# The context's four recurrence steps between the decays of later pieces, with weights loaded together and the recurrence placed ahead

## The chip, the cores and the metric

The kernel runs on one core of one Trainium2 chip. The metric is the device time of one execution in microseconds (us), taken as the median of several runs.

## The reference, cut to what matters

One layer of a diffusion backbone. A context of 256 tokens and a latent stream of 1024 tokens go through the same combined projection; its columns feed a short gated convolution and a bidirectional RWKV-7 recurrence. The recurrence runs over the context first, in both directions, and the latents start from the states that the context left:

```python
def wkv_scan(state0, r, decay, kk, b, v, k, reverse):
    def step(S, inp):
        r_t, w_t, kk_t, b_t, v_t, k_t = inp
        sa = jnp.einsum("bhvk,bhk->bhv", S, kk_t)
        S = (S * w_t[:, :, None, :] - sa[..., None] * b_t[:, :, None, :]
             + v_t[..., None] * k_t[:, :, None, :])
        return S, jnp.einsum("bhvk,bhk->bhv", S, r_t)
...
        hc = modulate(rms_norm(ctx, norm1_g[l]), csh1, csc1)
        out_c, ctx_states = mixer_block(hc, lp, (zero_state, zero_state), not last)
        hx = modulate(rms_norm(x, norm1_g[l]), sh1, sc1)
        out_x, _ = mixer_block(hx, lp, ctx_states, True)
        x = x + g1 * out_x
        hx = modulate(rms_norm(x, norm2_g[l]), sh2, sc2)
        x = x + g2 * conv_ffn(hx, lp, rows, GRID_W)
```

`mixer_block` multiplies the concatenation of the two groups' outputs by `w_out`; the kernel splits this product into the convolution's half and the recurrence's half.

## The kernel before, in words

All work is in float32, with the large products done as three products of a rounded part (hi) and a rest (lo). The 1280 tokens are ten tiles of 128: tiles 0 and 1 are the context, 2 to 9 the latents. The program has these stages.

1. Norms, modulation and the projections of k and v, until about 270 us.
2. **Decays and inversions.** Five pieces of two tiles each, in the order 0 (the context), 2, 8, 4, 6 (`decay_and_invert`). The function `decays` handles a piece in eight groups (four blocks of channels j, two directions d). A group is two small products for the decays (`plo`), a row of operations on VectorE, ScalarE and GpSimd that make the factors `arO` and `kbO`, eight matrix multiplications into two banks `px` (L601 of before; they are recorded as sixteen, and are counted as sixteen below when rows are meant and as eight when the program is meant), VectorE's four masked reads of them (L603, L605), four transposes `pt`, and writes to DRAM. Then `invert` turns the piece's triangular blocks into their inverses: thirty pairs of dependent VectorE operations (L670, L672), two block transposes (L676, L678), 256 tiny products (`pq`, `pr`) and a write to DRAM (`xa_dram`, L700). The remaining projections (r, the gate, the convolution group: 17 columns of 48 matrix multiplications `pj`, L354) stand between this work on TensorE. Their weights are split by ScalarE and GpSimd (`wlo`, L106), and the convolution's own arithmetic (`cu`, `cy`, L832 to L840) is on VectorE.
3. **The recurrence.** `steps` does one chunk of 64 tokens of both directions. It loads the chunk (`cxa`, `ckb`, `car`, `cxr`, `vu`: 2.3 MB for both directions of a latent step), forms the right-hand side `ry` on TensorE (L752, L760), copies it to `rh` (L762, ScalarE for one direction, VectorE for the other), multiplies by the inverse into `pu` (L771), copies that to `vu` (L775, L777), multiplies into `ps` (L783), adds to the state `S` on VectorE (L786, four times) and, for latents, adds the outputs (L792, L800, L802). GpSimd multiplies the state and the loaded `car` by decays (L764, L650). Four steps cover the context, sixteen (r = 0 to 15) the latents. The latent step r takes tile 2 + r // 2 forward and tile 9 - r // 2 backward, so steps 0 to 3 need pieces 2 and 8 alone, and step 4 is the first that needs pieces 4 and 6.
4. **Work between the phases of a step.** `fill` takes parts from a list: `conv_out` (64 parts of three matrix multiplications, `pco`, L898) in latent steps 0 to 9, then per tile `mix`, `outp` (`po`, L898) and `to_h2`. The table `SL` says how many parts stand after each of the four phases of a step. `behind` holds these parts back until the recurrence's latest instructions are issued. `conv_out` needs `w_out`'s first four blocks, made by `w_make` (one product by the gate on VectorE, L891, a copy on ScalarE, a difference on GpSimd, L893).
5. The gated MLP, from about 1022 us to the end.

Each engine works off its instructions in the order that the program fixes; where the code leaves the order open, the framework's scheduler has chosen it at build time from its own model and from priorities. DMAs go out in order on SP's queue. PSUM's banks are handed out by `Banks`; a buffer or bank that is taken again makes the new user wait for the last reader of the old.

Of the kernel before, what the change touches and what calls it, by code (L numbers as in the profile page):

```python
# [2 lines left out]

# [12 lines left out]
D = 1024  # L16
# [13 lines left out]
SL = ((3, 2, 0, 2),) * 10 + ((0, 1, 3, 4),) + ((4, 4, 4, 6),) * 5  # L30
# [5 lines left out]
IB = 2  # L36
XB, XT = 2, 3
PADC, PADM = 88, 80
# [4 lines left out]
B1 = ((4, 5, 1), (2, 3), (6, 7), (0,), (1,))  # L43
# [4 lines left out]
B4 = dict(pm=(5, 7), px=(0,), ph=(4,))  # L48
# [39 lines left out]
def hybrid_kernel(  # L88
# [97 lines left out]
    md.tile([128, PADM], F32, name="padm")  # L186
# [327 lines left out]
    sx = ExitStack()  # L514
    dq = sx.enter_context(tc.tile_pool(name="dq", bufs=2, side="left", reuse_waits="tile"))
# [103 lines left out]

    Sd = []  # L620
# [4 lines left out]
    zero = st.tile([128, 2], F32, name="zero")  # L625
    G.memset(zero, 0.0)
    yts, before = {}, [None, None]

    class Chunk:


        def __init__(self, pool, d, t, ch):
# [13 lines left out]
            else:  # L646
                self.ar = pool.tile([128, 4, 2 * CH], F32, name="car")[:, :, 0:CH]
# [75 lines left out]
    def steps(pool, pairs, pp, bufs, sl=(0, 0, 0, 0)):  # L723


        cx = []
        rh = pool.tile([128, 512], F32, name="rh", bufs=1)
# [16 lines left out]
        for _ in cx:  # L744
            ry = pp.tile([128, 4, 128], F32, name="ry", tag="ry", bufs=bufs)
            rys.append((ry, ry.rearrange("p j (e v) -> p (j e) v", e=2)))
# [10 lines left out]
        for (u, v0, u0, vu, S), (ry, ry8) in both:  # L757
# [4 lines left out]
            chain["AV"[u.d]] = (A.copy, V.tensor_copy)[u.d](rh[u0:u0 + 64], ryf)  # L762
            if u.pc is not None:
                chain["G"] = F2.tensor_tensor(out=S, in0=S, in1=u.pc.to_broadcast([128, 4, 128]), op=ALU.mult)  # L764
        fill(sl[0])
        pus = [pp.tile([128, 4, 128], F32, name="pu", tag="pu", bufs=bufs) for _ in cx]
        with turns():
            for h in range(8):
                for (u, v0, u0, vu, S), pu in zip(cx, pus):
                    o = pu.rearrange("p j (e v) -> p (j e) v", e=2)[u0:u0 + 64, h, :]  # L770
                    chain["PE"] = PE.matmul(o, u.xa[u0:u0 + 64, h, :], rh[u0:u0 + 64, 64 * h:64 * h + 64], start=True, stop=True)  # L771
        for (u, v0, u0, vu, S), pu in zip(cx, pus):
# [3 lines left out]
            else:  # L776
                chain["V"] = V.tensor_scalar(out=vu[u0:u0 + 64], in0=puf, scalar1=-1.0, scalar2=None, op0=ALU.mult)  # L777
        fill(sl[1])
        for u, v0, u0, vu, S in cx:

            ps = pp.tile([128, 4, 64], F32, name="ps", tag="pu", bufs=bufs)
            for h in range(8):
                chain["PE"] = PE.matmul(ps[64 * (h % 2):64 * (h % 2) + 64, h // 2, :], u.kbt[:, 64 * h:64 * h + 64], vu[:, 64 * h:64 * h + 64], start=True, stop=True)  # L783
            for e in range(2):
                r = slice(64 * e, 64 * e + 64)
                chain["V"] = V.tensor_tensor(out=S[r, :, r], in0=ps[r], in1=S[r, :, r], op=ALU.add)  # L786
        fill(sl[2])
        both = [z for z in both if z[0][0].has_y]
# [4 lines left out]
        for (u, v0, u0, vu, S), (ry, ry8) in both:  # L793
# [10 lines left out]
            if e_[1] == 2 and (first or t in (3, 4)):  # L804
                SY.dma_start(yd[t], e_[0])
        fill(sl[3])

    ppc = Banks(px=B1[0], pj=B1[1], pl=B1[2], pq=B1[3], ry=B1[4], pu=B1[4])
# [36 lines left out]

    def decay_and_invert(ti):
# [22 lines left out]
    h2p = sh2.enter_context(tc.tile_pool(name="h2p", bufs=1, side="left", reuse_waits="tile"))  # L869
    h2 = [[h2p.tile([128, 8, 512], F32R, name=f"h2{hf}{i}", tag=f"h2{hf}{i}") for i in range(2)] for hf in range(1)]  # L870
# [12 lines left out]
    def w_raw(k):  # L883
        raws_[k] = cp_.tile([128, D], F32, name="xo", bufs=XB)
        SY.dma_start(raws_[k], w_out[0, 128 * k:128 * k + 128, :])

    def w_make(k):
# [5 lines left out]
        G.tensor_tensor(out=hl[1], in0=raw, in1=hl[0].bitcast(F32), op=ALU.subtract)  # L893
# [140 lines left out]
    ppc = Banks(ry=B2[0], pu=B2[1])  # L1034
    w_raw(0)
    w_raw(1)
    for r in range(4):
# [208 lines left out]
```

## Time and profile before

| | us |
|---|---|
| median of three runs | 1712.62 |
| the three runs | 1712.07, 1712.62, 1720.13 |
| the profiled execution, its own time | 1711.73 |
| its span in the trace | 1710.0 |

In the profiled execution TensorE's matrix multiplications are busy 91% of the span, VectorE 68%, ScalarE 33%, GpSimd 34%. TensorE's records overlap, so a full share means that it was never without work, not that it ran at its peak. The shares differ much by stage, so the argument goes by stretches of the trace. All times of rows are counted from the span's start.

### The profile page before, as it was taken

What the parts mean: (1) busy time and instruction counts of PE and PEld (TensorE: products, weight loads), DVE (VectorE), ACT (ScalarE), POOL (GpSimd) and SP (SyncE); (2) the same over time, 40 slices, a digit from 0 to 9 for tenths busy, and PEclk for the clock granted to TensorE, in tenths of its full rate; (3) what the DMA queues carried; (4) which work ended last, traced back from release to release, by engine and by line L of the source; (5) the groups of instructions that cost most, each with busy time, mean ns of one, the idle gap of its engine ahead of it and who ended that gap; (6) DMA issues with size and microseconds to landing.
All of it is one profiled execution on the core that took longest, in us unless ns stands there. A gap on an engine that the chain in (4) does not pass through costs nothing.

```text
span 1710.0 us, 27259 instructions
## 1 busy us (share of the span) xinstructions
PE 1558.9 (91%) x10639; PEld 1260.8 (74%) x10639; DVE 1157.2 (68%) x1795; ACT 565.1 (33%) x994; POOL 578.4 (34%) x515
## 2 busy tenths in 40 slices
PE   7699999989899966799678889999999999999997
PEld 2588768867777756687566768888888888788886
DVE  4963525698999987444578777777777777446645
ACT  2654315544445323221123421211111111324323
POOL 2343312333343304533344422222222222545643
PEclk9799799998999875999789999999999999999999
DMA  9385527557576486988652311111111111533531
GB/s 311 113 281 178 180 76 219 160 154 243 173 236 214 127 256 208 320 248 274 214 164 73 116 49 49 50 46 45 46 50 50 50 49 50 172 112 123 165 95 61
DMA packets 233721, 247.97 MB, mean 145 GB/s; under 512 B 18547, under 2 KB 171720, under 8 KB 233592
## 3 DMA queue, kind: packets, MB, share of 16 engines
q1 hardware_dynamic: 233208, 246.07, 46.2%
q8 instruction: 84, 1.38, 0.3%
q14 instruction: 45, 0.37, 0.1%
q0 software_dynamic: 384, 0.15, 0.0%
HBM read 179.32 MB, written 66.85 MB: 144 GB/s over the span
## 4 chain that ended last, share of the span: by engine, by line
PE 64%; DVE 23%; DMA 6%; ACT 3%; issue 3%; SPq 1%; POOL 0%; DVEq 0%; ACTq 0%
PE pf L1099 26%; PE pf L1179 13%; PE pj L354 10%; DVE tmp L670 3%; DVE ti L672 3%; PE pco L898 2%; PE po L898 2%; DMA araw<-in_ada_w_dram 2%; DVE acc L1146 2%; PE ry L760 1%; DVE xrO L605 1%; PE ry L752 1%; DVE xa L603 1%; PE ps L783 1%; PE px L601 1%
## 5 line engine op out<-in xcount | busy, mean ns | idle before, releaser
L1099 PE MATMUL pf<-h,fhi 128*128 128x512 f32 x1408 | 385.9, 391 | 5.9 <-DVE act L1151 4.1
L1099 PEld LDWEIGHTS pf<-h,fhi 128*128 128x128 f32 x1408 | 265.7, 189 | 62.6 <-DVE act L1151 4.5
L354 PE MATMUL pj<-hx,whi 128*128 128x512 f32 (+1 forms) x976 | 302.5, 389 | 1.6 <-DVE hx L328 1.3
L1146 DVE SCALAR_TENSOR_TENSOR acc<-gp,prm,acc 128x1024 f32<-128x1024 f32 x176 | 273.0, 1553 | 6.0
L106 POOL TENSOR_TENSOR flo<-fraw,fhi 128x1024 fp32r<-128x1024 f32 x50 | 122.0, 2441 | 315.8 <-ACT fhi L105 315.8
L1099 PE MATMUL pf<-h,flo 128*128 128x512 f32 x704 | 224.9, 392 | 0.0
L354 PEld LDWEIGHTS pj<-hx,whi 128*128 128x128 f32 x976 | 184.6, 197 | 38.2 <-issue 4.4
L354 PE MATMUL pj<-hx,wlo 128*128 128x512 f32 (+1 forms) x488 | 189.5, 389 | 0.0
L1179 PE MATMUL pf<-dhi,ahl 128*128 128x512 f32 x640 | 163.0, 389 | 0.2 <-DVE ahl L1171 0.2
L1171 DVE TENSOR_TENSOR ahl<-act,ahl 128x512 fp32r<-128x512 f32 x44 | 86.2, 1969 | 101.5 <-ACT ahl L1170 101.5
L1099 PEld LDWEIGHTS pf<-h,flo 128*128 128x128 f32 x704 | 132.9, 189 | 27.7 <-POOL flo L106 0.2
L105 ACT CAST fhi<-fraw 128x1024 fp32r<-128x1024 f32 x50 | 52.6, 1053 | 265.8 <-issue 158.4
L1179 PEld LDWEIGHTS pf<-dhi,ahl 128*128 128x128 f32 x640 | 120.0, 188 | 25.5 <-DVE ahl L1171 0.6
L106 POOL TENSOR_TENSOR dlo<-fraw,dhi 128x1024 fp32r<-128x1024 f32 x40 | 98.5, 2467 | 93.7 <-ACT dhi L105 89.7
L106 POOL TENSOR_TENSOR wlo<-wraw,whi 128x1024 fp32r<-128x1024 f32 x26 | 63.2, 2431 | 165.1 <-ACT whi L105 165.0
L1144 DVE TENSOR_SCALAR acc<-gp,prm 128x1024 f32<-128x1024 f32 x22 | 42.6, 1938 | 98.2 <-ACT gp L1136 98.2
L354 PEld LDWEIGHTS pj<-hx,wlo 128*128 128x128 f32 x488 | 96.2, 197 | 17.3 <-issue 1.7
L1179 PE MATMUL pf<-dlo,ahl 128*128 128x512 f32 x320 | 89.1, 389 | 0.0
L601 PE MATMUL px<-arO,kbO 64*128 64x128 f32 (+1 forms) x640 | 64.1, 308 | 18.3 <-DVE xrO L605 12.5
L601 PEld LDWEIGHTS px<-arO,kbO 64*128 64x128 f32 x640 | 51.9, 206 | 35.1 <-issue 29.2
L105 ACT CAST dhi<-fraw 128x1024 fp32r<-128x1024 f32 x40 | 41.9, 1050 | 105.0 <-PE pf L1179 87.5
L764 POOL TENSOR_TENSOR S<-S,pcs 128x512 f32<-128x512 f32 x38 | 40.1, 1069 | 94.1 <-PE ry L760 93.9
(281 smaller groups left out, 2621.6 us busy)
## 6 DMA issues: line engine op xcount, KB each, us to landing
araw<-in_ada_w_dram SPq DMA_DIRECT2D x48, 512.0 KB, 5.5
fraw<-in_ffn_w_up_dram SPq DMA_DIRECT2D x46, 512.0 KB, 3.9
fraw<-in_ffn_w_down_dram SPq DMA_DIRECT2D x44, 512.0 KB, 3.7
wraw<-in_w_in_dram SPq DMA_DIRECT2D x26, 512.0 KB, 5.3
lu<-lu_dram SPq DMA_DIRECT2D x20, 512.0 KB, 5.3
kb_dram<-kbT SPq DMA_DIRECT2D x40, 256.0 KB, 3.1
xa_dram<-xa SPq DMA_DIRECT2D x20, 512.0 KB, 4.9
cxa<-xa_dram SPq DMA_DIRECT2D x40, 256.0 KB, 3.8
```

What stands on the lines that cost most here:

```text
L105: A.copy(hi, src)
L106: G.tensor_tensor(out=lo, in0=src, in1=hi.bitcast(F32), op=ALU.subtract)
L354: PE.matmul(p[:, :n], w[:, k, :], hsl(i, k, t0, n), start=(k == 0 and first), stop=(k == 7 and last))
L601: PE.matmul(px[:, ch, i, 0:w], kbO[r, i, 2 * ch:2 * ch + 2, :].rearrange("p s n -> p (s n)"), rhs, start=True, stop=True)
L670: V.tensor_tensor(out=tv, in0=ti[:, j + 1:32, j:j + 1].to_broadcast([128, m, j]), in1=ti[:, j:j + 1, 0:j].to_broadcast([128, m, j]), op=AL ...
L672: V.tensor_tensor(out=ti[:, j + 1:32, 0:j], in0=ti[:, j + 1:32, 0:j], in1=tv, op=ALU.add)
L898: m = PE.matmul(po, hl[:, a_, k, :], w[k][b_][:, sl], start=(k == 0 and f), stop=(k == 3 and l))
L1099: PE.matmul(pts[hf], w[:, k, :], h2[hf][i_][:, k, :], start=(k == 0 and f), stop=(k == 7 and l))
L1144: V.tensor_scalar(out=acc, in0=src, scalar1=wcol, scalar2=prm[:, P_FB + f:P_FB + f + 1], op0=ALU.mult, op1=ALU.add)
L1146: V.scalar_tensor_tensor(out=acc, in0=src, scalar=wcol, in1=acc, op0=ALU.mult, op1=ALU.add)
L1171: V.tensor_tensor(out=hl[:, 1, :], in0=asl, in1=hl[:, 0, :].bitcast(F32), op=ALU.subtract)
L1179: PE.matmul(pd[i], hl[:, a_, 128 * q:128 * q + 128], w[w_][:, 512 * nh:512 * nh + 512], start=(f == 0 and s_), stop=(f == NF - 1 and l_))
```

## The change

It computes the same with the same number of matrix multiplications and VectorE instructions. What differs:

- The four context steps are issued from `decay_and_invert`, two during piece 2 and two during piece 8 (at the sixth and fourteenth `yield` of a piece), with a ring `rc` of their own of two buffers. They are no longer a loop in front of the latent steps.
- The steps' instructions are built inside `tc.high_priority(offset=HP)`, the parts of `fill` outside it.
- The right-hand side is copied into the half of `vu` in which U will stand, so `rh` is gone. The two directions of a context step share banks; `zero` is a slice of `rst`.
- `px` has two banks (4, 5) in place of three (4, 5, 1), since banks 0 and 1 now also serve the context steps. `IB` is 1: the inversion has one buffer of each kind.
- All eight blocks of `w_out` are loaded after the last piece, six of them into the spare halves of `x2s`, and made after latent steps 0 to 3. GpSimd's difference is done in two halves. `SL` puts no parts into steps 0 and 1 and eight, not seven, into the following ones.
- The outputs of tiles 3 and 4 are no longer written to `y_dram` and read again. In the stages after step 9 `px` and `ph` alternate between banks 0 and 4.

```diff
-SL = ((3, 2, 0, 2),) * 10 + ((0, 1, 3, 4),) + ((4, 4, 4, 6),) * 5
+SL = ((0, 0, 0, 0),) * 2 + ((4, 2, 0, 2),) * 7 + ((4, 4, 0, 4),) + ((0, 1, 3, 4),) + ((4, 4, 4, 6),) * 5
-IB = 2
+IB = 1
+CS = (5, 13)
+HP = 400
-B1 = ((4, 5, 1), (2, 3), (6, 7), (0,), (1,))
+B1 = ((4, 5), (2, 3), (6, 7), (0,), (1,))
-B4 = dict(pm=(5, 7), px=(0,), ph=(4,))
+B4 = dict(pm=(5, 7), px=(0, 4), ph=(4, 0))
...
-            chain["AV"[u.d]] = (A.copy, V.tensor_copy)[u.d](rh[u0:u0 + 64], ryf)
+            chain["AV"[u.d]] = (A.copy, V.tensor_copy)[u.d](vu[u0:u0 + 64], ryf)
...
     def decay_and_invert(ti):
-        for _ in decays(ppc, (ti,)):
-            pass
-        for _ in invert(ppc, ti):
-            pass
+        for n, _ in enumerate(chainit(decays(ppc, (ti,)), invert(ppc, ti))):
+            if n in CS and before_y:
+                steps(rc, before_y.pop(0), ppc, 1)
...
+    before_y += [[(0, r // 2, r % 2), (1, 1 - r // 2, 1 - r % 2)] for r in range(4)]
     for ti in (2, 8, 4, 6):
         decay_and_invert(ti)
...
     def w_raw(k):
-        raws_[k] = cp_.tile([128, D], F32, name="xo", bufs=XB)
+        raws_[k] = [x2s[1][:, 2], x2s[1][:, 3], X2[1], X2[6], X2[2], X2[5], None, None][k]
+        if k > 5:
+            raws_[k] = cp_.tile([128, D], F32, name="xo", bufs=XB)
...
     def mix_load(t):
         y = yts[t, False][0]
-        if t in (3, 4):
-            y = op.tile([128, 512], F32, name="y", bufs=NY)
-            SY.dma_start(y, yd[t])
...
-    ppc = Banks(ry=B2[0], pu=B2[1])
-    w_raw(0)
-    w_raw(1)
-    for r in range(4):
-        steps(ring, [(0, r // 2, r % 2), (1, 1 - r // 2, 1 - r % 2)], ppc, 1)
-
-        with behind():
-            w_make(2 * r)
-            w_make(2 * r + 1)
-        if r < 3:
-            w_raw(2 * r + 2)
-            w_raw(2 * r + 3)
-        if r == 1:
-            pend.append(conv_out())
-            next(pend[0])
+    for k in range(8):
+        w_raw(k)
+    pend.append(conv_out())
+    next(pend[0])
     for r in range(16):
...
         steps(ring, [(0, 2 + r // 2, r % 2), (1, 9 - r // 2, 1 - r % 2)], pp, 2, SL[r])
+        if r < 4:
+            with behind():
+                w_make(2 * r)
+                w_make(2 * r + 1)
```

The order of the built programs shows where this puts the instructions. On TensorE before, the last projections (`pj`) stand at the last group of the last piece, and the first context step (`ry`, L752) follows the first products of its inversion:

```order
L601 MATMUL px<-arO,kbO 128x128 x7
L354 MATMUL pj<-hx,whi 128x512
L688 MATMUL pq<-rti,xa 32x32 x32
L609 MATMUL pt<-cst,kbO 128x128 x4
L354 MATMUL pj<-hx,wlo 128x512
L601 MATMUL px<-arO,kbO 128x128 x8
L688 MATMUL pq<-rti,xa 32x32 x32
L695 MATMUL pr<-xr,qs 32x32 x32
L752 MATMUL ry<-vu,cxa 64x64
```

In the change the last projections stand at the 23rd of the 40 groups, in piece 8, beside the third context step (L758, L766, and its `pu` at L781):

```order
L356 MATMUL pj<-hx,whi 128x512
L699 MATMUL pr<-xr,qs 32x32 x32
L605 MATMUL px<-arO,kbO 128x128 x7
L559 MATMUL plo<-dxl,lu 128x256
L560 MATMUL plo<-dxl,lu 128x256
L356 MATMUL pj<-hx,whi 128x512
L356 MATMUL pj<-hx,wlo 128x512
L758 MATMUL ry<-vu,cxa 64x64 x16
L766 MATMUL ry<-S_2053,car 64x128 x4
L613 MATMUL pt<-cst,kbO 128x128 x4
```

Counted over the whole order, 1,142 of the 1,464 projection multiplications stand ahead of the end of the 22nd group before, and 1,462 in the change; ahead of the end of the first group it is 729 in both. From the third group on, about 39 of them stand between two groups in the change, 16 to 20 before.

On VectorE at the end of the last inversion, before, the third context step's adds to the states (L786) stand inside it, and the fourth one's copy (L762) just behind it:

```order
L786 TENSOR_TENSOR S_2052<-ps,S_2052 64x4x64 x2
L672 TENSOR_TENSOR ti<-ti,tmp 128x2x29
L891 TENSOR_TENSOR xo<-xo,gb_6606 128x1024
L670 TENSOR_TENSOR tmp<-ti 128x30
L672 TENSOR_TENSOR ti<-ti,tmp 128x30
L676 STREAM_TRANSPOSE xr<-ti 128x32x32
L678 STREAM_TRANSPOSE rti<-ti 128x32x32
L891 TENSOR_TENSOR xo<-xo,gb_6606 128x1024
L681 COPY xa<-xr 32x32x32 x2
L762 COPY rh<-ry 64x512
```

In the change the step in the same place is latent step 3 (its copy L768 stands a few pairs ahead), so five more steps are done by then; the products by the gate (L914) come only behind it, and the next copy is that of step 4:

```order
L680 STREAM_TRANSPOSE xr<-ti 128x32x32
L682 STREAM_TRANSPOSE rti<-ti 128x32x32
L787 TENSOR_SCALAR vu<-pu 64x512
L685 COPY xa<-xr 32x32x32 x2
L800 TENSOR_TENSOR S_2053<-ps,S_2053 64x4x64 x2
L800 TENSOR_TENSOR S_2055<-ps,S_2055 64x4x64 x2
L914 TENSOR_TENSOR xo<-xo,gb_6989 128x1024 x2
L914 TENSOR_TENSOR x_6985<-x_6985,gb_6989 128x1024 x3
L768 COPY vu<-ry 64x512
```

On SP's queue in the change, six of the eight weight blocks (L908) stand behind the last inversion's writes (L704) and step 4's `cxa`; four blocks of `x` (L934) and then step 5's loads follow:

```order
L704 DMA xa_dram<-xa 128x1024 x4
L642 DMA cxa<-xa_dram 128x512 x3
L908 DMA x_6985<-in_w_out_dram 128x1024 x4
L908 DMA x_6984<-in_w_out_dram 128x1024 x2
L934 DMA x_6984<-in_x_dram 128x1024 x2
L934 DMA xo<-in_x_dram 128x1024 x2
L647 DMA car<-ar_dram 128x512 x2
```

Before, the blocks were loaded two at a time from about 616 us on, between the context steps' loads. The first `pco` stands behind step 4's states' products in the change, and behind step 0's before.

## Rows read from the trace of the kernel before

**Rows 1.** Busy time by stretch: PE, PEld, DVE, ACT, POOL, clock, DMA, GB/s.

```profile
270.00:325.00 55.00, 55.00 (x350) 44.74 (x349) 32.51 (x65) 27.27 (x55) 18.39 (x27) 1.00 0.61 184
325.00:458.00 133.00, 119.37 (x966) 97.33 (x964) 124.97 (x294) 64.18 (x118) 47.79 (x71) 0.91 0.60 178
458.00:611.00 153.00, 140.52 (x1296) 113.75 (x1296) 147.09 (x342) 71.43 (x138) 50.03 (x78) 0.95 0.62 190
611.00:663.00 52.00, 27.72 (x478) 24.43 (x477) 44.93 (x86) 13.60 (x18) 16.36 (x14) 0.60 0.90 271
663.00:811.00 148.00, 134.09 (x2146) 113.42 (x2145) 66.62 (x107) 37.05 (x61) 59.28 (x51) 0.92 0.86 271
811.00:1022.00 211.00, 168.45 (x1367) 134.69 (x1366) 148.38 (x262) 67.91 (x154) 80.71 (x70) 0.91 0.40 127
```

**Rows 2.** Timeline of TensorE at the first group: start, duration, what, count.

```profile
276.51 1.11 PE L601 MATMUL px<-arO,kbO 64*128 64x64 f32 x16
...
278.52 0.63 PE L354 MATMUL pj<-hx,whi 128*128 128x512 f32 x2
278.99 0.39 PE L354 MATMUL pj<-hx,wlo 128*128 128x512 f32 x1
279.21 0.63 PE L354 MATMUL pj<-hx,whi 128*128 128x512 f32 x2
```

**Rows 3.** Timeline of TensorE at the 22nd group and a later one.

```profile
456.04 2.04 PE L601 MATMUL px<-arO,kbO 64*128 64x128 f32 x14 [0.21 <-DVE xrO L605]
458.02 1.12 PE L609 MATMUL pt<-cst,kbO 128*128 128x128 f32 x4
...
466.36 1.16 PE L601 MATMUL px<-arO,kbO 64*128 64x128 f32 x16
467.45 0.66 PE L609 MATMUL pt<-cst,kbO 128*128 128x128 f32 x4
```

**Rows 4.** Timeline of VectorE at the end of the last inversion.

```profile
656.58 1.22 DVE L891 TENSOR_TENSOR xo<-xo,gb 128x1024 f32<-128x1024 f32 x1
...
660.81 1.99 DVE L678 STREAM_TRANSPOSE rti<-ti 128x1024 f32<-128x1024 f32 x1
```

**Rows 5.** Groups of VectorE, 325 to 600 us: count | busy us, mean ns | idle.

```profile
L836 DVE SCALAR_TENSOR_TENSOR cy<-cu,prm,cy 128x1024 f32<-128x1024 f32 x8 | 10.6, 1329 | 0.0
...
L832 DVE TENSOR_TENSOR cu<-pj,cu 128x512 f32<-128x512 f32 x8 | 5.5, 682 | 0.0
L834 DVE TENSOR_SCALAR cy<-cu,prm 128x1024 f32<-128x1024 f32 x4 | 5.1, 1270 | 0.0
L840 DVE TENSOR_TENSOR cy<-pj,cy 128x512 f32<-128x512 f32 x7 | 4.7, 678 | 0.0
```

**Rows 6.** Timeline of VectorE and GpSimd around 569.8 us.

```profile
569.07 0.38 DVE L670 TENSOR_TENSOR tmp<-ti 128x238 f32<-128x238 f32 x1
...
569.80 2.39 POOL L106 TENSOR_TENSOR wlo<-wraw,whi 128x1024 fp32r<-128x1024 f32 x1 [4.96 <-ACT whi L105]
...
569.93 2.52 DVE L670 TENSOR_TENSOR tmp<-ti 128x240 f32<-128x240 f32 x1
```

**Rows 7.** Timeline of a latent step on VectorE and GpSimd.

```profile
747.28 0.68 DVE L777 TENSOR_SCALAR vu<-pu 64x512 f32<-64x512 f32 x1 [0.77 <-PE pu L771]
748.34 2.06 POOL L650 TENSOR_TENSOR car<-car,pcs 128x512 f32<-128x512 f32 x2 [2.98 <-DMA car<-ar_dram]
749.54 1.78 DVE L786 TENSOR_TENSOR S<-ps,S 64x256 f32<-64x256 f32 x4 [1.57 <-PE ps L783]
```

**Rows 8.** Timeline of ScalarE: right-hand-side copies of latent steps 4, 5 and 10.

```profile
743.26 0.58 ACT L762 COPY rh<-ry 64x512 f32<-64x512 f32 x1 [2.63 <-PE ry L760]
...
754.72 0.58 ACT L762 COPY rh<-ry 64x512 f32<-64x512 f32 x1 [2.64 <-PE ry L760]
...
811.05 0.58 ACT L762 COPY rh<-ry 64x512 f32<-64x512 f32 x1 [6.33 <-PE ry L760]
```

**Rows 9.** The last inversion's last write on SP, and landing times (L700; page).

```profile
678.75 1.01 SPq L700 DMA_DIRECT2D xa_dram<-xa  x2
...
DMA to landing us min/median/max: 2.6/4.9/6.1
...
cxa<-xa_dram SPq DMA_DIRECT2D x40, 256.0 KB, 3.8
```

**Rows 10.** Waits from 800 to 1022 us: total, times, longest.

```profile
PE ry L752 <- DVE y L802: 18.9, 7, 9.9
...
DVE mu L959 <- DMA y<-y_dram: 5.9, 1, 5.9
```

More of the change, by code (lines that the diff above doesn't have):

```diff
@@ L2 @@
 from contextlib import ExitStack, contextmanager
+from itertools import chain as chainit
 import concourse.bass as bass
@@ L514, in hybrid_kernel @@
     sx = ExitStack()
+    rc = sx.enter_context(tc.tile_pool(name="rc", bufs=2, side="left", reuse_waits="tile"))
     dq = sx.enter_context(tc.tile_pool(name="dq", bufs=2, side="left", reuse_waits="tile"))
@@ L624, in hybrid_kernel @@
         Sd.append(S0)
-    zero = st.tile([128, 2], F32, name="zero")
-    G.memset(zero, 0.0)
+    zero = rst.rearrange("p (b t) -> p b t", t=CH)[:, 0:2, 0]
     yts, before = {}, [None, None]
@@ L743, in steps @@
         rys = []
-        for _ in cx:
-            ry = pp.tile([128, 4, 128], F32, name="ry", tag="ry", bufs=bufs)
+        for u, *_ in cx:
+            if u.has_y or not rys:
+                ry = pp.tile([128, 4, 128], F32, name="ry", tag="ry", bufs=bufs)
             rys.append((ry, ry.rearrange("p j (e v) -> p (j e) v", e=2)))
@@ L761, in steps @@
             ryf = ry[u0:u0 + 64].rearrange("p j n -> p (j n)")
-            chain["AV"[u.d]] = (A.copy, V.tensor_copy)[u.d](rh[u0:u0 + 64], ryf)
+            chain["AV"[u.d]] = (A.copy, V.tensor_copy)[u.d](vu[u0:u0 + 64], ryf)
             if u.pc is not None:
                 chain["G"] = F2.tensor_tensor(out=S, in0=S, in1=u.pc.to_broadcast([128, 4, 128]), op=ALU.mult)
+        hp.close()
         fill(sl[0])
-        pus = [pp.tile([128, 4, 128], F32, name="pu", tag="pu", bufs=bufs) for _ in cx]
+        hp.enter_context(tc.high_priority(offset=HP))
+        pus = []
+        for u, *_ in cx:
+            pus.append(pp.tile([128, 4, 128], F32, name="pu", tag="pu", bufs=bufs) if u.has_y or not pus else pus[0])
         with turns():
@@ L786, in steps @@
                 chain["V"] = V.tensor_tensor(out=S[r, :, r], in0=ps[r], in1=S[r, :, r], op=ALU.add)
+        hp.close()
         fill(sl[2])
+        hp.enter_context(tc.high_priority(offset=HP))
         both = [z for z in both if z[0][0].has_y]
@@ L803, in steps @@
             e_[1] += 1
-            if e_[1] == 2 and (first or t in (3, 4)):
+            if e_[1] == 2 and first:
                 SY.dma_start(yd[t], e_[0])
+        hp.close()
         fill(sl[3])
-    ppc = Banks(px=B1[0], pj=B1[1], pl=B1[2], pq=B1[3], ry=B1[4], pu=B1[4])
+    ppc = Banks(px=B1[0], pj=B1[1], pl=B1[2], pq=B1[3], ry=B1[3], pu=B1[4])
     def r_and_gate():
@@ L892, in w_make @@
         A.copy(hl[0], raw)
-        G.tensor_tensor(out=hl[1], in0=raw, in1=hl[0].bitcast(F32), op=ALU.subtract)
+        for i in range(2):
+            c = slice(512 * i, 512 * i + 512)
+            G.tensor_tensor(out=hl[1][:, c], in0=raw[:, c], in1=hl[0][:, c].bitcast(F32), op=ALU.subtract)
     def product(po, hl, w, sl):
```

19 lines of the change are left out of this document (13 added, 6 removed).

## The prediction

> **What bounds the kernel now.** I read the busy time by stretch first [rows 1]. From 270 to 611 us two engines are close to full at once: TensorE is busy 55.0 of 55, 119.4 of 133 and 140.5 of 153 us, VectorE 125.0 of 133 and 147.1 of 153 in the last two. These are the decays and inversions. VectorE carries them; the projections fill TensorE between the groups and are spread so evenly that both engines finish together. From 611 to 663 us (the last inversion with context steps 1 to 3) only VectorE has much to do, 44.9 of 52, and TensorE 27.7 at a granted clock of 0.60. Then the latent steps with `conv_out` keep TensorE at 134.1 of 148. From 811 to 1022 us neither is full (168.5 and 148.4 of 211): there the chain of step, mix and output product waits on itself. After that the MLP is bound by TensorE and begins as much earlier or later as its input comes, so the question is when the stretch before 1022 us ends.
>
> The change removes no arithmetic worth naming. It moves 320 projection multiplications, four context steps, four latent steps and `w_make` against each other, so I cost four stretches.
>
> **1. To the end of the 22nd group.** In the trace it begins at 276.5 us and ends at 458.0 with the last `px` product [rows 2, 3]. Up to there the order of before has 1,142 projection multiplications and the change 1,462, and both begin the stretch at 729. Three of them take 278.52 to 279.21, 0.23 us each [rows 2]; 320 more are 73.6 us. Two context steps come in as well. A latent step costs TensorE 754.72 - 743.26 = 11.46 us per round [rows 8], less 21 `pco` at the same 0.23 (4.8), so 6.6 us; without the output products I estimate 5.5 for a context step, 11 for two. What can absorb this is TensorE's idle time in the stretch, about 14 us in 325 to 458 [rows 1], and the slack inside its busy time: a group alone takes 278.52 - 276.51 = 2.0 us [rows 2], so 733 x 0.23 + 21 x 2.05 + about 8 for two inversions' products + 11 is only 231 us, against 181.5 now. That is +50 us if TensorE never waits and +85 if nothing is absorbed. TensorE in 270 to 325 was fed all the time and yet needed 55 us for 156 x 0.23 + 8 x 2.05 = 52.3, 5% over the sum; 231 x 1.05 = 243 gives +61. I take **+62**. VectorE cannot be the bound here, for it has the work of 181 us to do in 243.
>
> **2. From there to the end of the last inversion.** In the trace 458.0 to 662.8 (L678 ends) [rows 3, 4], 204.8 us, VectorE all but full. The change has the same 18 groups and three inversions left, but no projections. What leaves VectorE: the convolution's arithmetic, 25.9 us in 325 to 600 [rows 5], of which 322 of 576 columns' multiplications, 56%, belong to this stretch: 14.5. Three products by the gate at 1.22 [rows 4]: 3.7. Delay by GpSimd: a L670 of usually 0.4 us took 2.52 beside a weight split of 2.39 [rows 6], so 2.1 us for each of 6.7 splits of `wlo` and 3 of `wl`: 20. What comes: six steps instead of three, each 2 x 0.68 + 1.78 = 3.14 us of VectorE [rows 7], 9.4; GpSimd's four multiplications per step, 4.1 us [rows 7], 12.3 for three steps, of which I let VectorE feel 5, since not every operation stands beside one; and VectorE's waits for the steps, 7.1 us idle for three in 611 to 663 [rows 1], so 7 more. Together -38 + 21 = **-17**, from -29 (the steps cost only their own operations) to +5 (the splits cost nothing, all of GpSimd's new work does).
> The Trainium skill ("SBUF — State Buffer", Who interferes with whom) says that a VectorE instruction with two inputs in SBUF and a GpSimd instruction that reads SBUF exclude each other for the whole instruction. The 2.52 us agree; by that rule all 12.3 us would count, and the whole forecast would come out 7 us later.
>
> So the last inversion ends 62 - 17 = 45 us later, at about 708 us.
>
> **3. From there to step 10's right-hand side.** Before, 811.05 - 662.8 = 148.2 us [rows 8, 4]. In the change step 4 has to wait for piece 6: the last write went out at 679.8, 17 us after the inversion's end; it lands 4.9 us later, `cxa` takes 3.8 [rows 9], and the products and state terms of `ry` about 2.5: 28 us with TensorE mostly idle. Then 192 `pco` (44.2 us) and the six steps 4 to 9 (39.6) are all that is left, 84 us, where steps 0 to 9 were still to do before: 112 us. The other limit is DMA. Weights 3 MB, x 4 MB, seven steps' loads 16 MB, and about 6 MB of outputs and convolution tiles make 29 MB; at the 271 GB/s of 663 to 811 [rows 1] that is 107 us behind the last write, 124 in all. Six weight and four x blocks (5 MB) go out ahead of step 5's loads, which eats into TensorE's start but not into the sum. I take 114, close to TensorE's floor since part of the loads is in when the inversion ends: **-34**, between -36 and -24.
>
> **4. From step 10 to the MLP.** The outputs of tiles 3 and 4 came back from `y_dram`; L959 waited 5.9 us for them, and the state's next add (L802) behind it on VectorE held TensorE's L752 for up to 9.9 us, 18.9 in all [rows 10]. The 9.9 goes. The steps' operations now stand ahead of mix and output work on VectorE, and `px` and `ph` have two banks; of the other 9.0 us I take 3. **-13**, from -5 (only the wait for the data goes) to -25 (all of L802's waits, and more of VectorE's idle 62 us).
>
> Right-hand side in `vu`, single buffers in the inversion, `zero` in `rst`, the split in halves: nothing, for their readers are done long before the next writer, and the halves have the sum of the whole.
>
> **Sum:** +62 - 17 - 34 - 13 = -2 us on 1711.7, so 1709.7; the profiled execution lies 0.9 below the median, which makes about **1711 us**: no change that can be measured. A difference under 0.5%, 8.5 us, is about what these measurements cannot tell from none. The likeliest case by itself reaches from 1703 to 1720.
>
> **Rivals.**
> - *TensorE never waits in the first stretch* (+50, not +62): 1699. For it: it was busy in every slice of 270 to 325. Against: from 325 on it was idle for 10%, behind VectorE's reads, and a group now has two banks, not three. 18%.
> - *The tail opens up.* If the steps no longer wait in 811 to 1022, all of L802's 18.9 us and a share of VectorE's 62 us idle go, -25 instead of -13: 1699. It decides once step 10 to 15 take 17 us each. Against: the mixes of the last tiles then only stand closer together at the end. 19%.
> - *Half the clock with two banks* (the other side). From 520 to 708 us TensorE has little to do, as in 611 to 663, where it had 0.60. A group's `px` and `pt` took 2.0 and 1.1 us at the lower level (455 us) and 1.16 and 0.66 at the full one [rows 3]: 1.3 us for each of 18 groups, 23 us, but only if VectorE has nothing in between. With three banks it had; with two, the next `px` must wait for the reads of the group before. 1734. It decides when VectorE is idle over 1 us per group. The Trainium skill ("TensorE: Matmul & The Clock Gate", Part 1) names the same two levels and idling as the cause of the lower; the 0.60 agrees. 16%.
> - *All weights at once come too late.* 5 MB ahead of step 5's loads are 18 us at 271 GB/s; if the first `pco` also waits for blocks 2 and 3, TensorE stands still for 13 us more: 1724. 8%.
> - *The latent steps don't come early.* Their ring takes the space of the projections' operands; should its loads wait so long that steps 0 to 3 fall behind the last inversion, four rounds of 11.46 us come back, less 12 for VectorE's relief: 1745. Against: those operands are free earlier than before. 3%.
>
> **How the numbers follow.** Forecast 36%, which is the chance of no change; faster by over 0.5% the first two rivals, 37%; slower by over 0.5% the other three, 27%. The range goes from the two faster cases with the low bounds of terms 1 and 2 partly added (1684) to just over the clock's case (1737).
>
> **What would show it.** The last `pj` should stand near 520 us, the end of the 22nd group near 520, the last L682 near 708, step 4's copy (L768) near 736, the first `pco` beside it, step 10's copy near 822, no wait of L981 (the mean in `mix`) for `y`. VectorE should be about 70% busy up to 520 us and over 90% after, at a clock near 0.6 to 0.7. The forecast is wrong if TensorE's stretch ends before 500 us or VectorE's second takes under 170 or over 215.

## The result, and the profile after

The change makes the kernel slower: 1768.07 us (median of 4 runs, 1761.30 to 1770.66) against 1712.38 for the kernel before beside it (4 runs), a ratio of 1.0309 with a 95% interval of 1.0284 to 1.0333. The prediction, 1711 us and no measurable change, was wrong, and its range (to 1737) did not hold the time. The profiled execution took 1761.3 us, the lowest of the four, on a span of 1759.5.

Busy time by stretch after the change, over the same stretches as [rows 1] (columns as there):

```profile
270.00:325.00 55.00, 55.00 (x307) 44.73 (x307) 20.30 (x47) 26.52 (x49) 13.33 (x21) 1.00 0.50 152
325.00:458.00 133.00, 126.57 (x969) 101.02 (x968) 91.09 (x193) 52.46 (x94) 43.36 (x55) 0.99 0.55 165
458.00:611.00 153.00, 133.25 (x1188) 107.27 (x1189) 133.62 (x295) 55.84 (x106) 51.62 (x77) 0.83 0.68 204
611.00:663.00 52.00, 42.66 (x447) 35.81 (x448) 42.93 (x106) 23.96 (x45) 14.73 (x28) 0.53 0.62 193
663.00:811.00 148.00, 106.72 (x1604) 89.88 (x1602) 102.02 (x206) 50.39 (x80) 57.47 (x54) 0.72 0.70 226
811.00:1022.00 211.00, 174.62 (x1870) 139.96 (x1870) 138.88 (x260) 57.95 (x134) 85.80 (x74) 0.91 0.52 162
```

From 325 to 458 us VectorE is busy for 91 us, where it was 125. TensorE is now the only full engine there. From 663 to 811, where VectorE had 67 us to do, it has 102, and TensorE runs at a granted clock of 0.72 instead of 0.92. The two engines no longer finish together: first TensorE is the full one, then VectorE.

TensorE at the 22nd group and VectorE at the end of the last inversion, which answer to [rows 3] and [rows 4]:

```profile
546.85 1.16 PE L605 MATMUL px<-arO,kbO 64*128 64x128 f32 x14
...
548.51 0.39 PE L356 MATMUL pj<-hx,wlo 128*128 128x512 f32 x1
...
551.52 0.48 PE L605 MATMUL px<-arO,kbO 64*128 64x128 f32 x2
...
553.20 1.16 PE L605 MATMUL px<-arO,kbO 64*128 64x128 f32 x14
```

```profile
745.00 1.86 DVE L682 STREAM_TRANSPOSE rti<-ti 128x1024 f32<-128x1024 f32 x1
746.89 0.69 DVE L787 TENSOR_SCALAR vu<-pu 64x512 f32<-64x512 f32 x1
```

The 22nd group's px is done at 548 instead of 458, and the last pj stands right behind it (607.7 before). A group's 16 px come as 2 and 14 in 19 of the first 22 groups; before, 11 of them ran in one piece, as the later group in [rows 3]. The last inversion ends at 747 instead of 663. ScalarE's copies of the latent steps 4, 5 and 10 [rows 8]:

```profile
776.03 0.58 ACT L768 COPY vu<-ry 64x512 f32<-64x512 f32 x1
790.63 0.58 ACT L768 COPY vu<-ry 64x512 f32<-64x512 f32 x1 [3.90 <-PE ry L766]
...
867.27 0.58 ACT L768 COPY vu<-ry 64x512 f32<-64x512 f32 x1 [8.00 <-PE ry L766]
```

The four stretches of the forecast, then, against the profiled execution before:

| stretch | before, us | after, us | forecast | measured |
|---|---|---|---|---|
| to the 352nd px (from the first) | 181.5 | 273.4 (and begins 2 earlier) | +62 | +90 |
| to the end of the last inversion | 204.8 | 199 | -17 | -6 |
| to step 10's right-hand side | 148.2 | 120.3 | -34 | -28 |
| to the end of the execution's own time | 900.7 | 894.0 | -13 | -7 |
| sum | | | -2 | +50 |

The sign of each term was right. The first was 28 us short, and the other three each gave back less than was counted on. Neither of the two signs that the forecast named for being wrong appeared: TensorE's stretch did not end before 500 us, and VectorE's second took 199 us, between 170 and 215. No sign had been named for a first stretch that ends too late.

### The profile page after: what moved, and what is told of

It is laid out like the page before. It is cut to its first block, busy times and chain, and to the rows that moved or that the text cites. A ratio compares the mean times of both kernels' runs of the same rounds, so it can differ in the third digit from the quotient of the medians.

```text
span 1759.5 us, 27241 instructions
## 1 busy us (share of the span) xinstructions
PE 1598.3 (91%) x10639; PEld 1288.6 (73%) x10639; DVE 1156.5 (66%) x1795; ACT 570.2 (32%) x994; POOL 586.6 (33%) x522
## 4 chain that ended last, share of the span: by engine, by line
PE 46%; DVE 5%; DMA 2%; ACT 1%; issue 1%; POOL 0%; DVEq 0%; SPq 0%; ACTq 0%; POOLq 0%
PE pf L1114 25%; PE pf L1194 12%; PE po L923 3%; PE pco L923 2%; DVE acc L1161 2%; PE ry L766 1%; PE ry L758 1%; PE pu L781 1%; PE ps L797 1%; DVE rstd L178 0%; DVE acc L1159 0%; PE pg L998 0%; DMA fraw<-in_ffn_w_down_dram 0%; DMA y<-y_dram 0%; PE ry L808 0%
## 5 line engine op out<-in xcount | busy, mean ns | idle before, releaser
L605 PE MATMUL px<-arO,kbO 64*128 64x128 f32 (+1 forms) x640 | 79.6, 337 | 5.6 <-ACT kbT L615 3.7
L605 PEld LDWEIGHTS px<-arO,kbO 64*128 64x128 f32 x640 | 62.7, 228 | 21.9 <-issue 10.4
```

What stands on the lines that cost most here:

```text
L605: PE.matmul(px[:, ch, i, 0:w], kbO[r, i, 2 * ch:2 * ch + 2, :].rearrange("p s n -> p (s n)"), rhs, start=True, stop=True)
```

## The experiments

Each run was timed against the kernel before on the same chip. "Before" is then 1711 to 1716 us, and the ratios carry the comparison.

**What brings the projections forward, and what do the early steps do?** Theory: px on two banks instead of three decides where the projections stand, and that is the cost. Rivals: the early steps (1), the weights at once or the tail (2).

```
e1, kernel before:   B1 = ((4, 5, 1), (2, 3), ...  ->  B1 = ((4, 5), (2, 3), ...
e2, changed kernel:  B1 = ((4, 5), (2, 3), (6, 7), (0,), (1,))
                 ->  B1 = ((4, 5, 1), (2, 3), (6, 7), (0,), (0,))
e3, changed kernel:  CS = (5, 13) -> CS = (), and behind the loop over (2, 8, 4, 6):
+    while before_y:
+        steps(rc, before_y.pop(0), ppc, 1)
e4:                  the edits of e2 and e3 together
```

> The kernel before with one edit: px has banks 4 and 5 instead of 4, 5 and 1. Theory (two banks for px bring the projections forward): its order has 997 projection products by the 64th px and 1,453 by the 160th (before: 841 and 1,094), so TensorE is busy to about 540 us and VectorE alone after; the 22nd group ends near 535 (before 458.0: 320 more pj at the 0.244 us that each took between starts in 276 to 458, 78 us), the last L678 near 735 to 745, and the time is 1,755 to 1,775. Rival 1 (the early steps at high priority cost it): 1,707 to 1,717, because no step has moved. Rival 2 (the weights at once and the tail cost it): the same 1,707 to 1,717.

> The changed kernel with one edit: px gets bank 1 back as its third, and the four steps' pu and ps share bank 0 with pq and ry. All other parts of the change stay. Theory: the projections are spread again (841 by the 64th px, 1,077 by the 160th), the 22nd group ends at 465 to 480, the last L682 at 650 to 670, and the time is 1,675 to 1,705, under before, because the steps over the context are out of the end of that stretch and the latent steps need not wait for them. Rival 1: 1,750 to 1,770, since the steps stand where they stood in the change. Rival 2: 1,750 to 1,770.

> The changed kernel with the four steps over the context issued after the last inversion in the program, px on two banks as in the change. Theory: the projections stand as early as in the change (997 by the 64th px, 1,453 by the 160th), TensorE's first stretch is 10 us shorter for two steps less, and the rest gives it back: 1,750 to 1,770. Rival 1: 1,705 to 1,720, as before. Rival 2: 1,755 to 1,770.

> The changed kernel with both edits: px on three banks and the four steps after the last inversion in the program. What is left of the change is the single inversion buffers, the steps' high priority, the right-hand side in vu, the weights at once behind the first four latent steps, the outputs of tiles 3 and 4 not reloaded and two banks each for px and ph in the tail. Theory: 1,690 to 1,712, the tail's 5 to 13 us kept and the first stretch as before. Rival 1: the same. Rival 2: 1,750 to 1,770.

Measured: e1 1767.1 us (1.0310, 1.0283 to 1.0337), e2 1743.2 (1.0170, 1.0141 to 1.0199), e3 1817.7 (1.0605), e4 1776.9 (1.0367). The single edit of e1 costs as much as the whole change. Its 352nd px begins at 535.9 us and its last L678 at 740.7, as the theory had it; both rivals fall as the whole explanation. But the theory does not stand alone either: with three banks the change is still 1.7% slower than before, where 1,675 to 1,705 us was expected. There is a second cost. (The edit of e2 also moves the steps' pu and ps to bank 0, which pq and ry use, so their sharing is part of what e2 measures.)

e3 and e4 are spoiled by their own edit. The steps behind the last inversion share bank 0 with pq, and their ry stood in TensorE's queue behind it. TensorE's waits from 640 to 700 us in e4 (total, times, longest):

```profile
PE pq L692 <- DVE rti L682: 31.0, 1, 31.0
```

The first of their copies came at 687.9 us, 4 us behind the inversion's last write; before it came at 630.3. They say nothing on early steps; e11 below puts the steps on banks of their own.

**Single buffers, the bank of pu, the tail.**

```
e5, kernel before:   IB = 2 -> IB = 1
e6, e2 and:          xb, ti, rti, xr, qs from one ring, tag="iv", bufs=3 (rti allocated ahead of xr)
e7, changed kernel:  B1 = ((4, 5, 1), (2, 3), (6, 7), (0,), (1,))
e8, kernel before:   B4 = dict(pm=(5, 7), px=(0, 4), ph=(4, 0)); e_[1] == 2 and first;
                     mix_load without the load of y for tiles 3 and 4
```

> The kernel before with one edit: the inversion's tiles have one buffer instead of two (as in the change). The version with three banks for px but all else of the change took 1,743 us, 28 us over before, 46 us of it between the 22nd group and the last inversion, where VectorE stood 5.2 us before an xb for the pr products of the inversion ahead. Theory (single buffers are the second cost of the change): each inversion after the first begins later by 5 to 15 us, the last L678 ends at 680 to 700 (before 662.8), and the time is 1,735 to 1,755. Rival (the early steps cost it: their instructions stand in VectorE's queue, or their pu and ps share a bank with pq): 1,708 to 1,718, because no step has moved.

> The changed kernel with three px banks and with the same three inversion buffers used in turn (xb, ti, rti, xr, qs through one ring of three): the next inversion's xb now waits for the pq products of the one ahead, not for its pr, which come up to 14 us later. Theory (single buffers): the last L682 moves from 713 towards 680 and the time falls from 1,743 to 1,700 to 1,725. Rival (the early steps themselves): it stays at 1,735 to 1,750.

> The changed kernel with three px banks, and the steps' pu and ps on bank 1, which px uses too, instead of on bank 0 with pq. Its order brings the projections forward from the first step on (1,266 by the 160th px against 1,077 with pu on bank 0). Theory (the order of the projections follows the free banks, and standing early costs time): 22nd group's end at 485 to 510 and 1,745 to 1,765. Rival (what costs there is that pu and ps share a bank with the inversion's pq): under 1,735, since pq is free of them.

> The kernel before with the tail's part of the change alone: the outputs of tiles 3 and 4 are not written out and read back, and px and ph have two banks in the tail. The forecast gave these parts and the steps' priority together 13 us (5 to 25). Theory (the removed 9.9 us of L802 are given back in the next wait, as the change measured only 6.7): 1,704 to 1,711. Rival (the wait was the whole cost and the change lost it again elsewhere): 1,698 to 1,703. Rival (nothing): 1,711 to 1,717.

Measured: e5 1719.4 us (1.0043, 1.0026 to 1.0060), e6 1738.4 (1.0149, 1.0111 to 1.0186), e7 1757.8 (1.0267), e8 1709.9 (0.9986, 0.9967 to 1.0005). Single buffers cost 0.4%, about a quarter of what was expected of them, although in e5 the last L678 begins 40 us later (701.0): steps run ahead of it in the meantime, and step 10 is only 14 us late. Their use in turn wins back 0.2% at most (the intervals of e2 and e6 overlap). In e7 px has three banks, one of them shared with pu, and the time is 1.0% above e2's: the projections come forward here too (1,266 by the 160th px against 1,077), and VectorE waits 26.2 us for px and 8.1 for pt from 275 to 660 us, where e2 shows 18.3 and no wait for pt. So a bank that is often taken acts in part like one that is missing. The tail's parts are worth nothing that this measurement tells from zero. In e8 the wait for y is gone, and the other waits of the steps stay; TensorE's waits from 809 to 1022 us there, beside [rows 10]:

```profile
PE ry L752 <- DVE y L802: 8.3, 5, 5.2
PE ps L783 <- DVE vu L777: 6.2, 3, 3.0
PE pu L771 <- DVE rh L762: 5.9, 5, 3.6
PE ry L752 <- DMA car<-ar_dram: 4.2, 1, 4.2
```

**The clock, and the rest of the change.** e9 tests the forecast's rival of half the clock; e10 to e12 start from e6, the best version with early steps so far.

```
e9, changed kernel, ahead of kbT in decays:
+                    if ti in (4, 6):
+                        fl = pp.tile([128, 4, 128], F32, name="fl", tag="pu", bufs=1)
+                        for i in range(28):
+                            PE.transpose(fl[:, i % 4, :], ident, ident)
e10, e6 and:  HP = 400 -> HP = 0
e11, e6 and:  CS = (); ahead of the latent steps, on ppc = Banks(ry=(2, 3), pu=(1, 6)):
+    for s_ in before_y:
+        steps(ring, s_, ppc, 1)
e12, e6 and:  w_raw two at a time behind the latent steps 0 to 2, conv_out queued after step 1
```

> The changed kernel (two banks, 1,768 us) with work added that nothing reads: 28 transposes of the identity, 128x128, per group of the last two pieces, on the bank of pu, 448 in all. They stand behind the last projection, in the stretch of 548 to 747 us, where TensorE's granted clock is 0.65 and VectorE waits 14.5 us for px and pt (1.6 in the kernel before). Theory (half the clock is part of the cost there, and low only because TensorE lacks work): the granted clock of that stretch rises above 0.85, VectorE's wait for px and pt falls under 6 us, the last L682 moves from 745 to 733 to 741, and the time is 1,755 to 1,765. Rival (the clock is no cost, or the added 0.13 us each delay px as much): 1,766 to 1,785, the last L682 at 745 or later.

> The version with three px banks and the inversion's buffers in turn (1,738 us), the steps without their priority. Its order has the same projections and the same places of the steps over the context up to the 256th px. Theory (the early place of the steps costs, not their priority): 1,732 to 1,744. Rival (priority makes VectorE and ScalarE wait in order for the steps' products: VectorE stands about 5 us for them, and db and sw 10 us behind ScalarE): 1,715 to 1,728.

> The same version (1,738 us) with the four steps over the context issued where the kernel before has them, from the ring and on banks 2, 3, 1 and 6, ahead of the latent steps; all weights are still loaded at once. Its order of projections is that of the kernel before. Theory (the early steps cost what is left, some 20 us): 1,708 to 1,722. Rival (the weights at once cost it: behind them the products of conv_out begin 51 us later than before): 1,730 to 1,750.

> The same version (1,738 us) with early steps, but the weight blocks loaded two at a time behind the first four latent steps and conv_out queued after the second, as the kernel before does at its four steps over the context. Theory (early steps cost, weights at once do not): 1,738 to 1,760, since the second half of the blocks now comes later. Rival (weights at once cost it, by holding the steps' own loads): 1,715 to 1,730.

Measured: e9 1785.3 us (1.0412, 1.0389 to 1.0435), e10 1730.2 (1.0099, 1.0066 to 1.0131), e11 1728.1 (1.0077, 1.0050 to 1.0104), e12 1738.3 (1.0141, 1.0112 to 1.0169). In e9 the granted clock of 548 to 747 us rose from 0.65 to 0.87, and VectorE's wait for px and pt rose as well, from 14.5 to 21.6 us. The 448 transposes stood ahead of px in the queue, so the run does not tell what the clock alone costs. Priority costs some 0.5% in e10, though its interval overlaps that of e6; the early steps, with the bank that they share with pq, some 0.7% in e11, half of what was left to explain. The way in which the weights are loaded is worth nothing that shows.

**Place of the projections or the banks' own waits?** e13 and e14 keep two banks and hold the projections back, and e18 holds them with three. e15 and e16 take the rest of the change apart.

```
e13, changed kernel, and e14, e1 (gm: the last px of each group, in program order):
+    def hold():
+        if len(gm) < 40:
+            return ExitStack()
+        nseg[0] += 1
+        return tc.issue_after(gm[7 + (nseg[0] - 1) * 32 // 26].ins)
...
         for (t0, n), p in zip(segs, pts):
+            with hold():
e15, e11 and:  w_make(2 * r), w_make(2 * r + 1) behind the steps over the context
e16, e15 and:  HP = 0, SL = ((3, 2, 0, 2),) * 10 + ...
e17, kernel before:  B1 = ((4, 5, 1, 3), (2,), (6, 7), (0,), (1,))
e18, kernel before:  hold() alone, px on its three banks
```

> The changed kernel (two px banks, 1,768 us) with one addition: each of the last 26 half rows of projections (24 products each) is queued on TensorE behind the px of a later group, so that they spread over groups 8 to 40: 840 by the 64th px, 1,004 by the 128th, 1,152 by the 192nd (kernel before: 841, 998, 1,150). Nothing waits for more than its place in the queue. Theory (the place of the projections is the cost): the 22nd group ends at 455 to 485 instead of 547.7, the last L682 at 700 to 725, and the time is that of three banks, 1,735 to 1,750. Rival (two banks cost by their own waits, px held by VectorE's reads of the group before): the 22nd group ends over 490 and the time is 1,755 to 1,785.

> The kernel before with two px banks (1,767 us alone) and the same holding of the projections. Theory: 1,710 to 1,725, as with three banks. Rival (the two banks' own waits): 1,735 to 1,770.

> The version without early steps (three banks, buffers in turn; 1,728 us) with w_make back behind the four steps over the context instead of behind the first four latent steps. All blocks are still loaded at once, and the steps keep their priority. It came to step 10's right-hand side 169 us after the last inversion, 150 in the kernel before, and its first pco at 731, 706 before. Theory (w_make behind the latent steps is what costs there): the first pco at 700 to 712, step 10 at 808 to 818, 1,706 to 1,718. Rival (the priority or the loading at once costs it): 1,722 to 1,732.

> The same without the steps' priority, and with the output products spread over the steps as the kernel before has them. What is left of the change is the single buffers in turn, the right-hand side in vu, the weights loaded at once and the tail's parts. Theory (w_make): 1,704 to 1,716, no better than the run with priority by more than 5 us. Rival (the priority costs): 1,704 to 1,716 here, but 1,722 to 1,732 with it.

> The kernel before with bank 3 given from the projections to px: px on 4, 5, 1 and 3, pj on bank 2 alone. Its order has 951 projection products by the 128th px and 1,363 by the 320th (998 and 1,464 before), so some 100 are left behind the last group. Theory (px's waits for banks still cost VectorE 20 us with three): the wait for px falls under 8 us, the last L678 moves from 661 to 645 to 655, 1,700 to 1,709. Rival (one bank holds up the projections, whose every block must be read before the next): 1,715 to 1,745.

> The kernel before, px on its three banks, with the holding of e13 and e14 alone (984 projection products by the 128th px, 1,131 by the 192nd, 1,441 by the 320th; before 998, 1,150 and 1,464). Theory (the 2.0% of e14 are the two banks): 1,708 to 1,720. Rival (the holding costs it): 1,730 to 1,750.

Measured: e13 1755.1 us (1.0258, 1.0243 to 1.0274), e14 1745.7 (1.0200, 1.0183 to 1.0216), e15 1726.2 (1.0096, 1.0081 to 1.0111), e16 1715.1 (1.0019, 1.0008 to 1.0030), e17 1728.0 (1.0084, 1.0053 to 1.0116), e18 1718.3 (1.0029, 1.0012 to 1.0045). e14 answers the main question against both pure forms: two banks alone cost 3.1% (e1); with the projections about as evenly spread as before (1,080 by the 160th px, 1,094 before) they still cost 2.0%, of which the holding itself is 0.3% (e18). So more than half of it, some 1.7%, comes with two banks even when the projections are spread, and the rest with their early place. VectorE's waits from 275 to 660 us, in the kernel before, the changed kernel and e14 (total, times, longest):

```profile
DVE xa L603 <- PE px L601: 20.0, 10, 4.8
DVE db L579 <- ACT da L559: 4.3, 4, 1.4
```

```profile
DVE kbO L584 <- PE pt L613: 46.6, 17, 4.7
DVE xa L607 <- PE px L605: 32.1, 14, 4.6
```

```profile
DVE kbO L589 <- PE pt L619: 32.9, 14, 4.7
DVE xa L613 <- PE px L610: 20.9, 11, 6.0
```

The wait for pt is new with two banks, and is there in e14 too, 32.9 us. With three banks (4, 5, 1) a group's two px and its pt each have a bank of their own. With two, pt takes the first px's bank and must wait until VectorE has read it. The transposes then come late, and VectorE can't write kbO for a later group until pt has read the old one. e2, with three banks and the rest of the change, has no wait for pt among its seven largest, and waits 18.3 us for px.

What makes pt late stands in TensorE's order as well. A group of e14 on TensorE, and VectorE beside it:

```profile
391.45 2.07 PE L610 MATMUL px<-arO,kbO 64*128 64x128 f32 x14
...
394.47 1.06 PE L363 MATMUL pj<-hx,whi 128*128 128x512 f32 x2
...
398.13 1.20 PE L705 MATMUL pr<-xr,qs 32*32 32x32 f32 x64
399.26 0.66 PE L619 MATMUL pt<-cst,kbO 128*128 128x128 f32 x4
```

```profile
393.50 0.41 DVE L615 TENSOR_TENSOR xrO<-px,cst 128x256 f32<-128x256 f32 x1
...
399.96 0.42 DVE L589 TENSOR_TENSOR kbO<-db,sw 128x256 f32<-128x256 f32 x1 [4.15 <-PE pt L619]
```

The first px has been read at 393.9 us, but 12 pj, from 394.5 us on, and the pr still stand ahead of pt, and VectorE waits 4.15 us for it. Counted over the first 22 groups, no pj stands between a group's last px and its pt in the kernel before (as in [rows 3]) and in e2, and on the mean 14 do in e14 and 16 to 17 in e1 and the change; pt then starts about 5 us behind px instead of at once. In e1 and the change these are about as many pj as come forward. So the wait for pt and the early projections seem to have one source, the projections that the scheduler puts where pt has to wait for its bank. No run puts pt right behind px on two banks, so how much of the 1.7% is this order, and how much the wait for the read itself, is not shown. From 548 us on, where the change has no pj left, TensorE itself stands before pt until VectorE has read a px (TensorE's waits from 548 to 747 us):

```profile
PE pt L613 <- DVE xrO L609: 13.8, 9, 2.6
```

The granted clock is lower too, 0.83 from 275 to 709 us in e14 against 0.91 from 273 to 650 in e18, and no run parts what that costs from the waits.

e16 against e15 puts the priority and the new `SL` together at 0.8%; without these and the early steps what is left of the change costs 0.2%. e17 was the attempt at a version ahead of both kernels: the last L678 began 12 us earlier (648.6), but the single bank of pj left projections until 645 us, the first sum of a pco came at 730.5 (706.1 before), and VectorE still waited 21.7 us for px. No version here is shown to beat the kernel before.

## Why the prediction was wrong

**The step that failed** is the sum of term 1: "733 x 0.23 + 21 x 2.05 + about 8 for two inversions' products + 11 is only 231 us", which was raised by 5% to +62, with +85 named as the bound "if nothing is absorbed". The time of TensorE from each start to the next, less idle, in the trace (us, and count; before 276.5 to 458.0, after 274.3 to 547.7):

```
            before           after
pj          100.7 (413)      178.7 (733)
px           33.1             32.5
pt           11.1             11.8
plo          13.1             14.3
pbn           3.2              4.1
pq, pr        6.6              9.1
steps         0               12.0
idle         13.6             10.8
sum         181.4            273.3
```

A group was priced too low. Its 2.05 us come from the first group [rows 2], whose 2.0 us from px to the next pj hold these rows beside its px:

```profile
277.55 0.66 PE L609 MATMUL pt<-cst,kbO 128*128 128x128 f32 x4
277.96 0.36 PE L555 MATMUL plo<-dxl,lu 128*128 128x256 f32 x1
...
278.40 0.28 PE L556 MATMUL plo<-dxl,lu 128*128 128x256 f32 x1
```

That is a group of the context: its px have 64 columns and come in one piece, and it has no pbn. The 22 groups of the changed stretch took 62.7 us (px, pt, plo and pbn in the table), 2.85 each, where 43 were counted: 20 more. A pj took 0.244 us from start to start, not 0.23, which is 10 more. The steps (12.0 against 11) were right, and the 5% (12) covers the idle time (10.8). Nothing was absorbed. By the forecast's own prices the old stretch would hold 146 us of work (413 x 0.23 + 21 x 2.05 + 8), and TensorE worked in it for 168: the "slack inside its busy time" was the rest of the groups' and the pj's cost. So 320 more pj at 0.244 are 78, with the steps 90, and the stretch grew by 92. The upper bound, 320 x 0.23 + 11, was too low as well, mainly by the price of a pj.

**Term 2** had the right parts and wrong prices. VectorE's work fell from 192.0 us (458 to 663) to 178.7 (548 to 747), by 13 where the forecast's parts give 24. GpSimd's splits were to give 20 of it. The 90 multiplications of the three inversions, on which the forecast had read that delay, before and after:

```profile
L670 DVE TENSOR_TENSOR tmp<-ti 128x30 f32<-128x30 f32 (+14 forms) x90 | 43.3, 481 | 1.8
```

```profile
L674 DVE TENSOR_TENSOR tmp<-ti 128x30 f32<-128x30 f32 (+14 forms) x90 | 35.6, 395 | 1.9
...
L607 DVE TENSOR_TENSOR xa<-px,cst 128x256 f32<-128x256 f32 x38 | 15.8, 417 | 9.8 <-PE px L605 9.7
...
L584 DVE TENSOR_TENSOR kbO<-db,sw 128x256 f32<-128x256 f32 x17 | 8.9, 523 | 4.9 <-PE pt L613 4.8
```

That is 7.7 us less, net of what GpSimd's work for the steps adds. From 458 to 663 us the trace has eight splits (five of `wlo`, three of `wl`), not 9.7. An estimate of the delay, from each VectorE operation there set against the fastest of its line and shape, is 11 us beside the eight splits, 1.4 us each: the 2.52 us of [rows 6] was one full collision, and not every split met one. Beside the steps' multiplications on GpSimd the same estimate is 5 us before and 14 after, 9 more where 5 were let in. The upper end of this term's range, +5, was also added up too low: its parts give +10. The waits were forecast at 7 more, and idle time did rise from 13.0 to 20.3. But they are waits for px and pt (14.5 us), not for the steps (3.5). This is the place and the point ("VectorE is idle over 1 us per group" is nearly met, 14.5 us for 18 groups) of the rival of half the clock, which was priced at 23 us. The granted clock there is 0.65, as it said. Whether the clock or the bank makes px late in this stretch stays open: e9 raised the clock and delayed px by its own work.

**Term 3** came close (-28 against -34), for a reason that was not the one given. e1 moves no step and loads no weight early, and still goes from the start of its last L678 (740.7) to step 10 (864.7) in 124 us, against 150 from the same start in the kernel before; e5 takes 124 too. When the last inversion is late, steps over the context and latent steps run ahead of it in any case. So this gain is the late inversion given back, and not something that the moved steps bring. With the inversion at its old place, e11 and e16 take 169 and 164 us.

**Term 4**: the wait for y went, as forecast, and half of the gain with it. TensorE's waits from 867 to 1075 us in the changed kernel, beside [rows 10]:

```profile
PE ph L1037 <- DVE xt L1025: 14.1, 3, 9.7
PE pu L781 <- DVE vu L768: 6.4, 3, 3.8
PE ry L758 <- DVE y L818: 6.0, 5, 2.6
```

L818, the old L802, holds ry for 6.0 us instead of 18.9, and ph now waits 14.1 us for xt, for which it did not wait before. So much of the wait moved to another place of the tail; e8 shows the parts by themselves at -0.1%, with zero inside its interval.

**Of the rivals**, "TensorE never waits" was nearly right in its premise (10.8 us idle in 273) and had the same wrong sum under it. "Half the clock with two banks" named the mechanism, the next px waiting for the reads of the group before, but placed it behind 520 us and priced it by the clock. The loss of the bank acts in the whole stretch, by pt more than by px.

**How the change adds up**, as a ladder of versions in ratios to the kernel before. Each step is a difference of two measured ratios, good to 0.2 to 0.5%:

| version | ratio | what the step adds |
|---|---|---|
| e16: buffers in turn, right-hand side in vu, weights at once, tail | 1.0019 | 0.2% |
| e15: and priority, with the new `SL` | 1.0096 | 0.8% |
| e11: and w_make behind the latent steps | 1.0077 | nothing that shows |
| e6: and the four steps early, on bank 0 with pq | 1.0149 | 0.7% |
| e2: and single buffers as in the change | 1.0170 | 0.2%, within the intervals |
| e13: and two banks for px, pu on bank 1, projections held | 1.0258 | 0.9%, of it 0.3% the holding by e18 |
| the change: and projections early | 1.0309 | 0.5% |

In the ladder two banks cost 1.4% in all, 0.6% with the projections held and up to 0.8% for their place. On the kernel before they cost more, 1.7% (e14 less e18) and up to 1.4% (e1 less that). The costs do not simply add. Why priority and early steps cost what they do was not followed to a wait; e2 shows VectorE standing 10.4 us for one pj and 5.4 us before xb for the pr of the inversion ahead, and that is all that was read of it.

The Trainium skill ("Perfetto Trace Analysis", Matmuls) advises that independent matmul groups rotate through different PSUM banks, so that the reading of one group overlaps the next one's products. The trace agrees: the wait for pt appears, at 46.6 us, with the third bank gone. The forecast weighed the loss of the bank as a cause of a lower clock, and did not ask what it does to pt.

## What to carry to other kernels

Price a unit of work by summing every instruction between its start and the next unit's over the whole stretch, and see that the sum gives back the old time, before "slack" is counted on: here 146 of 168 us. When a tile group has as many tiles as it has banks, taking one away makes one tile wait for the reader of another; look at what the order puts into that wait (here a run of projections) and at who then waits behind it (here VectorE, for a buffer that the late pt still had to read). And a gain that shows behind a delayed stretch may be only the delay given back; a run that has the delay and not the change tells.

## What the runs showed of the hardware

Two sizes were not expected. 28 small transposes per group took the granted clock of 548 to 747 us from 0.65 to 0.87 (e9), and the kernel became 1% slower than the change, not faster. And a GpSimd split cost VectorE about 1.4 us on the mean by the estimate above (11 us beside eight splits), where the one in [rows 6] had cost 2.1.
